# Moving part of the attention epilogue of a hybrid decoder layer between VectorE, ScalarE and TensorE

## The chip, the core and the metric

The kernel runs on one core of a Trainium2 chip. The metric is device time in microseconds (us) of one execution; lower is better. Three executions of the kernel before were timed, and one more was taken with the hardware profiler. The engines are named PE (TensorE), ACT (ScalarE), DVE (VectorE), POOL (GpSimd) and SP (SyncE, which here only issues transfers).

## The reference

A decoder layer over a sequence of 1024 tokens with model width 1024 computes a SwiGLU half-step, then a mixing step, then a second SwiGLU half-step, all with RMS norms before and after and with shift, scale and gate taken from a conditioning vector. The change lies in the mixing step, cut here to what matters:

```python
attn = sliding_window_attention(q, k, v, sinks)        # 8 query heads, 2 key heads, window 128
    # scores + bias; m = max(scores, sink); p = exp(scores - m)
    # p = p / (sum(p) + exp(sink - m));  out = p @ v
ssm = s5_ssm(u, ...)                                   # diagonal complex state space model, GELU, GLU
mixed = concat([rms_norm(attn, g_attn_out), rms_norm(ssm, g_ssm_out)])
mixed = mixed @ w_out
x = x + ga2 * rms_norm(mixed, g_post_mix)
```

The norm of attention's output needs, for each token, the sum of the squares of its 512 attention columns. It is a scale of the token's row, so it can be applied after the product with w_out.

## The kernel before, in words

Everything is float32. A large product is written as three TensorE products of rounded halves: `split` (lines 69 and 70) makes a high half with a ScalarE copy and a low half with a VectorE subtraction, and `mm3` (lines 74 to 76) adds high*high, high*low and low*high into one PSUM bank. So nearly every operand that PE reads in a `mm3` has passed through ACT first and DVE second.

The mixing step (`mix`) treats the tokens in 8 tiles of 128. For attention, tile t passes through three functions that are called one step apart. `at(n)` calls `at_values(n - 3)`, then `at_turn(n - 2)`, then `at_scores(n)`.

- `at_scores(t)`: 16 score products per tile on PE (line 841); 8 fused add, maximum and store operations on DVE, one per head (line 851); 8 exponentials on ACT with their sums (line 860); the reciprocal of the sums on DVE (lines 861, 862); and 8 scalings of the 128x256 probabilities by that reciprocal on DVE (line 864).
- `at_turn(t)`: 16 transposes on PE (line 875) into four PSUM banks, each split into halves (lines 69, 70 by way of line 877).
- `at_values(t)`: the products with v (lines 74 to 76, by way of line 889), their squares on ACT into the tile `sq` (line 890), and copies of the output on ACT (line 892). DVE then sums the four squares of a column (line 894), one PE product with a column of ones sums over the partitions (line 896), and DVE copies the result into one column of `ss_a` (line 897).

After the last tile (in `more`, line 1057) `rstd_a` is made from `ss_a` through a short chain on DVE and ACT (lines 141 to 145, 151), and the attention output and attention's share of w_out are split (lines 740 and 741 for w_out, which come through the stream `late`). `out_a(t)` multiplies tile t by attention's share of w_out in two halves of 512 columns and scales each half by `rstd_a` on DVE as it leaves PSUM (line 1048). In between stand the four quarters of the state space model: `ss_state(q)` (lines 978 to 1005; its two scans are lines 992 and 993, and half of its last products run on POOL) and `ss_out(q)` (lines 1016 to 1029).

PSUM has eight banks. The mixing step gives them out in turn (`mb`), in the order in which the program is written, so that a function's bank becomes free only when its user of eight allocations before has been read out.

The order of the instructions on each engine is not the order of the text. A planner in the framework goes through the program at build time with estimates of its own for what each operation takes, and puts on each engine's queue what is ready then, earlier text first. Only the long loops of the two SwiGLU half-steps have an order that is written out by hand (`pinned`). On the chip each engine takes its own queue in that order.

Of the kernel before, what the change touches and what calls it, by code (L numbers as in the profile page):

```python
# [15 lines left out]
MUL, ADD, SUB, MAX, MIN = ALU.mult, ALU.add, ALU.subtract, ALU.max, ALU.min  # L16

P = 128
# [12 lines left out]
def tile_layer(ctx: ExitStack, tc: tile.TileContext, a: dict, out: bass.AP, stage: str = "all"):  # L31
    nc = tc.nc
    pe, act, dve, pool, sp = nc.tensor, nc.scalar, nc.vector, nc.gpsimd, nc.sync
# [10 lines left out]
    def slot(tag, shape, dt=F32):  # L44
        uid[0] += 1
        return sb.tile([P] + list(shape), dt, tag=tag, name=f"{tag}_{uid[0]}")

    def bank(tag, shape=(512,)):
        uid[0] += 1
        return ps.tile([P] + list(shape), F32, tag=tag, name=f"{tag}_{uid[0]}")  # L50

    def small(n, name):
        uid[0] += 1
        return sm.tile([P, n], F32, tag=f"s_{name}_{n}", name=f"s{uid[0]}")
# [10 lines left out]
    def names(c, *idx):  # L65
        return tuple(f"{c}{i}" for i in idx)
# [5 lines left out]
    def mm3(psum, wh, wl, xh, xl, first, last, goes_on=False):  # L72

        pe.matmul(psum, wh, xh, start=first, stop=False, skip_group_check=goes_on)  # L74
        pe.matmul(psum, wh, xl, start=False, stop=False, skip_group_check=goes_on)  # L75
        pe.matmul(psum, wl, xh, start=False, stop=last, skip_group_check=goes_on)  # L76
# [26 lines left out]
    ones = cp.tile([P, 2], F32, name="ones")  # L103
# [6 lines left out]
    rstd_a, rstd_s, ss_a = (cp.tile([P, 8], F32, name=x) for x in ("rstd_a", "rstd_s", "ss_a"))  # L110
# [600 lines left out]

    AT = (1, 1, 0, 1, 0, 1, 0, 1, 0, 1, 0, 1)


    mb = Rot(*names("b", *range(8)))

# [47 lines left out]
    def mix(hm, st, st_u, late, shares, todo, start):  # L764
# [65 lines left out]
        def at_scores(t):  # L830
            nk = 1 if t == 0 else 2
            p2 = [slot(x, [2, 2, 256]) for x in (("a26", "a27"), ("a17", "c0"))[t % 2]]
            pr = {4 * kv + m: p2[m // 2][:, kv, m % 2] for kv in range(2) for m in range(4)}
            mx = small(8, "mx")
            ks = slice((2 - nk) * P, 256)
            for mp in range(2):
                pb = [bank(mb(), [2, 256]) for _ in range(2)]
                for m in (2 * mp, 2 * mp + 1):
                    for kv in range(2):
                        rows = slice(64 * kv, 64 * kv + 64)  # L840
                        pe.matmul(  # L841
                            pb[kv][:, m % 2, ks],
                            qT[m][rows, t * P : (t + 1) * P],
                            kT[rows, (t + 1 - nk) * P : (t + 1) * P],
                            start=True,
                            stop=True,
                        )
                for kv in range(2):
                    for m in (2 * mp, 2 * mp + 1):
                        hd = 4 * kv + m  # L850
                        dve.tensor_tensor_reduce(
                            pr[hd][:, ks], pb[kv][:, m % 2, ks], bias[kv][:, m, ks], 1.0, sink[:, hd : hd + 1],
                            ADD, MAX, mx[:, hd : hd + 1],
                        )
            nm, sm_, es = small(8, "nm"), small(8, "sum"), small(8, "es")
            dve.tensor_scalar(nm, mx, -1.0, None, op0=MUL)
            dve.tensor_tensor(es, sink, mx, op=SUB)
            act.activation(es, es, AF.Exp)
            for hd in range(NH):
                act.activation(pr[hd][:, ks], pr[hd][:, ks], AF.Exp, bias=nm[:, hd : hd + 1], accum_out=sm_[:, hd : hd + 1])  # L860
            dve.tensor_tensor(sm_, sm_, es, op=ADD)
            dve.reciprocal(sm_, sm_)
            for hd in range(NH):
                dve.tensor_scalar(pr[hd][:, ks], pr[hd][:, ks], sm_[:, hd : hd + 1], None, op0=MUL)
            A[t] = pr

        def at_turn(t):
# [11 lines left out]
        def at_values(t):  # L879
            nk = 1 if t == 0 else 2  # L880
            pr = A.pop(t)
            tk = slice(t * P, (t + 1) * P)
            sq = slot("t0", [4, P])
            for kv in range(2):
                rows = slice(64 * kv, 64 * kv + 64)
                po = bank(mb(), [4, P])
                for b in range(2 - nk, 2):
                    vb = t - 1 + b
                    mm3(po.rearrange("p m q -> p (m q)"), v_hi[:, vb, :], v_lo[:, vb, :], *pr[kv, b], b == 2 - nk, b == 1)
                act.activation(sq[rows], po[rows], AF.Square)  # L890
                for m in range(4):
                    act.copy(ag[m][rows, tk], po[rows, m, :])
            s1 = slot("t1", [P])
            dve.tensor_reduce(s1, sq.rearrange("p m q -> p q m"), op=ADD, axis=mybir.AxisListType.X)
            pc = bank(mb(), [2])
            pe.matmul(pc[:, 0:1], s1, ones[:, 0:1], start=True, stop=True)
            dve.tensor_copy(ss_a[:, t : t + 1], pc[:, 0:1])

        def ss_load(q):
# [13 lines left out]
        def at(n):  # L913

            if 3 <= n < NT + 3:
                at_values(n - 3)
            if 2 <= n < NT + 2:
                at_turn(n - 2)
            if n < NT:
                at_scores(n)  # L920
# [117 lines left out]
        acc = []  # L1038

        def out_a(t):  # L1040
            acc.append(slot(("r1", "r2", "r3", "a8", "c0", "a4", "a5", "a6")[t], [D]))
            tk = slice(t * P, (t + 1) * P)
            for dh in range(2):
                dk = slice(dh * 512, dh * 512 + 512)
                pb = bank(mb())
                for m in range(4):
                    mm3(pb, mix_a[0][m][:, tk], mix_a[1][m][:, tk], wo[m][0][:, dk], wo[m][1][:, dk], m == 0, m == 3)
                dve.tensor_scalar(acc[t][:, dk], pb, rstd_a[:, t : t + 1], None, op0=MUL)  # L1048

        wo, mix_a = [], []  # L1050

# [25 lines left out]
        while n < NT + 3:  # L1077
            n = more(n)
        ss_state(3)
        out_a(0)  # L1080
        out_a(1)
        ss_out(2)
        y_split(0)
        y_split(1)
        out_a(2)
        out_a(3)
        ss_out(3)
# [16 lines left out]
        for m in range(4):  # L1104
            gh, gl = late.get(4 + m)
            for hf in range(2):
                tk = slice(hf * 512, hf * 512 + 512)
                pb = bank(mb())
# [617 lines left out]
```

## Time and profile before

| what | us |
|---|---|
| median of the three timed executions | 1684.39 |
| lowest and highest of them | 1682.94 and 1687.2 |
| the profiled execution: its own time | 1682.71 |
| the profiled execution: its span, first to last instruction | 1680.9 |
| mixing step, attention and state space model, about | 740 to 960 of the span |

The mean granted clock of PE over the span is 0.993 of full speed. In the rows below, busy time is time in which the engine executes; an idle time in square brackets stands before the row's first instruction, with the engine, tile and line that ended it. Names such as `h` or `a` are the program's slots without their number; `b` are the PSUM banks.

### The profile page before, as it was taken

The numbers are of one execution on the slowest core, as the hardware profiler recorded it, in microseconds if no ns is written. First come the engines' busy times: TensorE is split into PE (matmuls) and PEld (weight loads), VectorE is DVE, ScalarE is ACT, GpSimd is POOL, SyncE is SP. The second block draws the span as 40 slices with busy tenths as digits, with TensorE's granted clock in tenths as the row PEclk, the third lists the DMA queues.
The fourth block names the chain that finished last, engine by engine and source line by source line (L and its number), as shares of the span: only waits on it lengthen the run. The fifth ranks groups of instructions, "written<-read, shape, count | busy, mean of one in ns | idle before, by whom it ended". The sixth has DMA issues, their size and how long they took to land.

```text
span 1680.9 us, 22023 instructions
## 1 busy us (share of the span) xinstructions
PE 1642.0 (98%) x7669; PEld 1349.3 (80%) x7669; DVE 1245.1 (74%) x2359; ACT 803.1 (48%) x1642; POOL 69.2 (4%) x119
## 2 busy tenths in 40 slices
PE   5999999999999999999989999999999999999998
PEld 4888888877788888888767887888888888888886
DVE  7999997889869768755589387777665666679585
ACT  5633333553345458736574268533333333355462
POOL 0011100001100000000013000000000000000000
PEclk8999999999999999999989999999999999999999
DMA  9176752234496334530232135352322233493344
GB/s 381 47 277 230 250 191 95 98 141 153 135 319 238 118 117 156 193 113 13 93 97 76 63 113 189 105 181 96 107 94 94 101 125 105 168 360 113 107 135 141
DMA packets 111056, 249.07 MB, mean 148 GB/s; under 512 B 11976, under 2 KB 27632, under 8 KB 110944
## 3 DMA queue, kind: packets, MB, share of 16 engines
q1 hardware_dynamic: 101216, 214.12, 36.9%
q0 software_dynamic: 9152, 32.49, 5.7%
q8 instruction: 60, 0.98, 0.2%
q10 hardware_dynamic: 576, 1.05, 0.2%
q14 instruction: 52, 0.43, 0.1%
HBM read 187.87 MB, written 59.75 MB: 147 GB/s over the span
## 4 chain that ended last, share of the span: by engine, by line
PE 89%; DVE 7%; ACT 2%; issue 1%; DMA 1%; SPq 0%; DVEq 0%; ACTq 0%
PE b L76 27%; PE b L75 27%; PE b L74 27%; PE b L841 1%; PE b L929 1%; PE b L931 1%; PE b L930 1%; PE b L875 1%; DVE h L495 1%; DVE w L70 1%; PE b L1020 0%; DVE h L532 0%; DVE a L166 0%; PE b L207 0%; ACT q L1431 0%
## 5 line engine op out<-in xcount | busy, mean ns | idle before, releaser
L75 PE MATMUL b<-a,w 128*128 128x512 f32 x1260 | 492.0, 390 | 3.4 <-DVE a L70 3.4
L76 PE MATMUL b<-a,w 128*128 128x512 f32 x1260 | 492.2, 391 | 1.0 <-DVE w L70 0.8
L74 PE MATMUL b<-a,w 128*128 128x512 f32 x1260 | 488.8, 391 | 3.9 <-ACT h L536 2.2
L74 PEld LDWEIGHTS b<-a,w 128*128 128x128 f32 x1260 | 236.9, 188 | 56.5 <-ACT h L536 3.8
L75 PEld LDWEIGHTS b<-a,w 128*128 128x128 f32 x1260 | 237.1, 188 | 52.5 <-DVE a L70 3.8
L76 PEld LDWEIGHTS b<-a,w 128*128 128x128 f32 x1260 | 237.1, 188 | 51.9 <-DVE w L70 3.0
L70 DVE TENSOR_TENSOR w<-r,w 128x512 fp32r<-128x512 f32 (+1 forms) x208 | 144.1, 694 | 129.9 <-ACT w L69 129.6
L75 PE MATMUL b<-w,r 128*128 128x512 f32 x528 | 205.5, 389 | 0.0
L76 PE MATMUL b<-w,r 128*128 128x512 f32 x528 | 205.4, 389 | 0.0
L74 PE MATMUL b<-w,r 128*128 128x512 f32 x528 | 183.5, 389 | 0.0
L69 ACT CAST w<-r 128x512 fp32r<-128x512 f32 (+1 forms) x208 | 129.1, 623 | 95.0 <-DVE r L397 82.4
L69 ACT CAST r<-a 128x512 fp32r<-128x512 f32 x110 | 68.5, 623 | 144.9 <-PE b L76 105.8
L70 DVE TENSOR_TENSOR r<-a,r 128x512 fp32r<-128x512 f32 x110 | 75.8, 689 | 73.6 <-ACT r L69 73.3
L74 PEld LDWEIGHTS b<-w,r 128*128 128x128 f32 x528 | 99.1, 188 | 20.7
L75 PEld LDWEIGHTS b<-w,r 128*128 128x128 f32 x528 | 99.1, 188 | 20.7 <-DVE w L70 0.2
L76 PEld LDWEIGHTS b<-w,r 128*128 128x128 f32 x528 | 99.1, 188 | 20.5
L69 ACT CAST w<-t 128x512 fp32r<-128x512 f32 (+1 forms) x114 | 69.9, 613 | 78.8 <-DVE t L400 32.3
L70 DVE TENSOR_TENSOR w<-t,w 128x512 fp32r<-128x512 f32 (+1 forms) x114 | 77.8, 682 | 34.4 <-ACT w L69 34.4
L532 DVE TENSOR_TENSOR h<-h,b 128x512 f32<-128x512 f32 x120 | 82.2, 685 | 20.4 <-PE b L76 18.6
L520 ACT ACTIVATE h<-h 128x512 f32<-128x512 f32 x60 | 38.0, 633 | 117.8 <-DVE h L532 117.8
L70 DVE TENSOR_TENSOR w<-a,w 128x512 fp32r<-128x512 f32 x110 | 75.3, 684 | 0.0
L74 PE MATMUL b<-a,a 128*128 128x512 f32 x182 | 71.3, 395 | 0.8 <-DVE r L1048 0.7
(393 smaller groups left out, 2475.2 us busy)
## 6 DMA issues: line engine op xcount, KB each, us to landing
r<-in_w_gu SPq DMA_DIRECT2D x87, 512.0 KB, 4.2
g_d<-h SPq DMA_DIRECT2D x154, 256.0 KB, 2.1
a<-g_d SPq DMA_DIRECT2D x110, 256.0 KB, 2.8
q<-in_w_ada POOLq DMA_DIRECT2D x48, 512.0 KB, 4.6
a<-in_w_d SPq DMA_DIRECT2D x88, 256.0 KB, 5.4
a<-in_w_ada SPq DMA_DIRECT2D x24, 512.0 KB, 9.6
a<-in_x SPq DMA_DIRECT2D x12, 512.0 KB, 6.1
x_d<-a SPq DMA_DIRECT2D x12, 512.0 KB, 3.5
```

Of the source, the lines that this page charges most:

```text
L69: act.copy(hi, src)
L70: eng.tensor_tensor(lo, src, hi.bitcast(F32), op=SUB)
L74: pe.matmul(psum, wh, xh, start=first, stop=False, skip_group_check=goes_on)
L75: pe.matmul(psum, wh, xl, start=False, stop=False, skip_group_check=goes_on)
L76: pe.matmul(psum, wl, xh, start=False, stop=last, skip_group_check=goes_on)
L495: dve.tensor_tensor(d, x, y, op=op)
L520: act.activation(dst, src, AF.Silu)
L532: dve.tensor_tensor(dst, dst, pb, op=ADD)
L841: pe.matmul(pb[kv][:, m % 2, ks], qT[m][rows, t * P : (t + 1) * P], kT[rows, (t + 1 - nk) * P : (t + 1) * P], start=True, stop=True,)
L875: pe.transpose(pt[:, m, :], pr[4 * kv + m][:, b * P : (b + 1) * P], ident)
L929: pe.matmul(pb, hh, wh, start=k == 0, stop=False)
L930: pe.matmul(pb, hh, wl, start=False, stop=False)
```

## The change

There are three edits. For the last two attention tiles (6 and 7) the 8 scalings of the probabilities are issued on ACT and not on DVE. For the same two tiles the DVE sum over the four squares is gone: PE takes the four 128x128 blocks of `sq` itself, in four products with the column of ones that add up in one bank. And in `out_a`, for all eight tiles, the first half of 512 columns (dh = 0) is scaled by `rstd_a` on ACT; the second half stays on DVE.

```diff
+    LATE = 6
...
             for hd in range(NH):
-                dve.tensor_scalar(pr[hd][:, ks], pr[hd][:, ks], sm_[:, hd : hd + 1], None, op0=MUL)
+                if t < LATE:
+                    dve.tensor_scalar(pr[hd][:, ks], pr[hd][:, ks], sm_[:, hd : hd + 1], None, op0=MUL)
+                else:
+                    act.mul(pr[hd][:, ks], pr[hd][:, ks], sm_[:, hd : hd + 1])
...
-            s1 = slot("t1", [P])
-            dve.tensor_reduce(s1, sq.rearrange("p m q -> p q m"), op=ADD, axis=mybir.AxisListType.X)
             pc = bank(mb(), [2])
-            pe.matmul(pc[:, 0:1], s1, ones[:, 0:1], start=True, stop=True)
+            if t < LATE:
+                s1 = slot("t1", [P])
+                dve.tensor_reduce(s1, sq.rearrange("p m q -> p q m"), op=ADD, axis=mybir.AxisListType.X)
+                pe.matmul(pc[:, 0:1], s1, ones[:, 0:1], start=True, stop=True)
+            else:
+                for m in range(4):
+                    pe.matmul(pc[:, 0:1], sq[:, m, :], ones[:, 0:1], start=m == 0, stop=m == 3)
...
-                dve.tensor_scalar(acc[t][:, dk], pb, rstd_a[:, t : t + 1], None, op0=MUL)
+                if dh:
+                    dve.tensor_scalar(acc[t][:, dk], pb, rstd_a[:, t : t + 1], None, op0=MUL)
+                else:
+                    act.mul(acc[t][:, dk], pb, rstd_a[:, t : t + 1])
```

## Rows read from the trace of the kernel before

**Rows 1.** The page's first part: busy time, share of the span, instructions.

```profile
PE 1642.0 (98%) x7669; PEld 1349.3 (80%) x7669; DVE 1245.1 (74%) x2359; ACT 803.1 (48%) x1642; POOL 69.2 (4%) x119
```

**Rows 2.** Busy time by stretch; after POOL: PE's granted clock, DMA share, GB/s.

```profile
850.00:860.00 10.00, 10.00 (x80) 7.11 (x77) 7.41 (x28) 6.25 (x21) 0.00 (x0) 1.00 0.01 5
860.00:870.00 10.00, 6.57 (x44) 4.54 (x42) 10.00 (x19) 9.86 (x33) 1.54 (x1) 0.86 0.46 155
870.00:880.00 10.00, 8.65 (x30) 6.39 (x31) 10.00 (x22) 3.75 (x12) 4.46 (x5) 0.62 0.29 93
880.00:890.00 10.00, 10.00 (x64) 7.97 (x64) 9.78 (x14) 6.38 (x11) 0.93 (x3) 1.00 0.18 47
...
910.00:920.00 10.00, 9.26 (x68) 7.50 (x67) 10.00 (x17) 1.96 (x3) 4.02 (x5) 1.00 0.01 2
...
1020.00:1050.00 30.00, 26.27 (x129) 20.64 (x128) 20.34 (x43) 27.55 (x50) 0.00 (x0) 1.00 0.54 192
```

**Rows 3.** Timeline of PE: start, us, engine, line, then idle time before it.

```profile
863.94 0.66 PE L875 MATMUL b<-ident,a 128*128 128x128 f32 x4
865.46 0.38 PE L896 MATMUL b<-ones,t 128*128 128x1 f32 x2 [0.86 <-DVE t L894]
867.78 0.80 PE L74 MATMUL b<-h,a 128*128 128x512 f32 x1 [1.94 <-ACT h L69]
868.75 0.79 PE L74 MATMUL b<-h,a 128*128 128x512 f32 x1 [0.18 <-ACT h L69]
871.35 0.80 PE L75 MATMUL b<-h,a 128*128 128x512 f32 x1 [1.80 <-DVE h L70]
...
918.70 0.50 PE L74 MATMUL b<-a,a 128*128 128x512 f32 x1 [0.74 <-DVE r L1048]
```

**Rows 4.** Single microseconds: length, PE busy, PE's granted clock, DMA share, GB/s.

```profile
866.00:867.00 1.00, 0.00 (x0) 1.00 0.98 389
867.00:868.00 1.00, 0.22 (x1) 0.64 0.86 344
...
877.00:878.00 1.00, 1.00 (x6) 0.74 0.00 0
```

**Rows 5.** The chain that ended last, in order of time.

```profile
852.25 0.31 PE b L896 x2
...
859.40 1.93 DVE a L864 x7
...
868.90 1.19 DVE s L861
```

**Rows 6.** Timeline of ACT, columns as in Rows 3.

```profile
854.92 0.58 ACT L69 CAST h<-b 128x512 fp32r<-128x512 f32 x1
859.25 1.15 ACT L740 ACTIVATE a<-a,cols 128x1024 fp32r<-128x1024 f32 x1 [3.75 <-DVE s L851]
...
866.53 0.49 ACT L860 ACTIVATE c<-c,s 128x256 f32<-128x256 f32 x1
866.93 0.18 ACT L860 ACTIVATION_READ_ACCUMULATOR c<-c,s 128x1 f32 x1
867.14 2.05 ACT L69 CAST h<-b 128x512 fp32r<-128x512 f32 x4
...
918.03 1.28 ACT L1023 ACT_TABLE_LOAD   x1 [11.18 <-PE b L1020]
```

**Rows 7.** Timeline of DVE, columns as in Rows 3.

```profile
857.66 0.19 DVE L862 RECIPROCAL s<-s 128x8 f32<-128x8 f32 x1
...
871.22 0.18 DVE L862 RECIPROCAL s<-s 128x8 f32<-128x8 f32 x1
...
893.18 1.07 DVE L894 TENSOR_REDUCE t<-t 128x128 f32<-128x512 f32 x1 [1.85 <-ACT t L890]
```

**Rows 8.** Instructions of lines 894 and 1048: shortest, median, longest (ns), first and last start.

```profile
L894 DVE TENSOR_REDUCE t<-t x8: 1020/1042/1070, 779.2 to 893.2; 128x128 f32<-128x512 f32 x8
...
L1048 DVE TENSOR_SCALAR a<-b,rstd_a x8: 750/750/751, 928.1 to 958.7; 128x512 f32<-128x512 f32 x8
```

## The prediction

> **What bounds the kernel now.** I read the busy shares first. PE is busy for 98% of the span and no other engine for more than 74% [rows 1], so work taken from DVE or given to ACT counts only where it moves a moment at which PE stands still, or where PE's own work grows.
>
> Next I split the mixing step into stretches of 10 us, to find those moments [rows 2]. From 850 to 860 PE is full at clock 1.00. From 860 to 880 it is not: 3.43 and 1.35 us idle, at granted clocks of 0.86 and 0.62, while DVE is busy for all 20 us. From 880 PE is full again, except for one gap of 0.74 us between 910 and 920. So there is one hole here, at 864 to 878, and one pinhole.
>
> PE's timeline says what the hole waits for [rows 3]. PE ends tile 6's transposes at about 864.6; it then waits 0.86 us for tile 5's sum of squares (line 894), 1.94 and 0.18 us for the high halves of tile 6's probabilities (line 69 on ACT), and 1.80 us for the first low half (line 70 on DVE). That is 4.78 us, until 871.35. Reading single microseconds [rows 4], the clock is still 1.00 in the idle microsecond 866 to 867, changes inside 867 to 868 (mean 0.64), and is back during 877 to 878 (mean 0.74). Its lower level of 1.2 GHz thus holds until about 877.5; from 871.35 that is 6.15 us of busy PE at half of 2.4 GHz, or 3.1 us lost on top of the wait.
>
> The chain of waits runs through DVE up to 871.35, and tile 6's scalings stand in it with 1.93 us for seven of the eight [rows 5]. On ACT the same stretch is a different picture [rows 6]: idle for 3.75 us up to 859.25, then in one run through w_out's first scaling (line 740), tile 5's read-out, tile 7's exponentials and, last, tile 6's four casts, which start only at 867.14 although the transposes were done by 864.6. Both engines are therefore close to setting the end of the hole.
>
> **The change, part by part.** The sum is made against the profiled execution's 1682.71 us and carried to the median, 1684.39, which is 1.68 above it.
>
> *Tile 6's scalings.* DVE loses 8 x 0.276 = 2.2 us (1.93 over seven) [rows 5]. ACT gains eight operations on 128x256; the trace has none of the kind, and the nearest are the exponentials of that size, which step by 0.40 us up to the readback of the sum, and by about 0.5 with it, as the exponential lasts [rows 6]. A plain multiplication has no readback, so I take 0.40, 3.2 us in all, and keep 4.1 (8 x 0.51, a cast of twice the size) as the upper end. The scalings can start when the reciprocal is done, at 857.85 [rows 7], inside ACT's idle time, and would end at 861.05. Of their 3.2 us, 1.40 lie in the hole up to 859.25 and 1.8 push what follows. Queued behind them on ACT are line 740, tile 5's read-out, tile 7's exponentials and tile 6's casts; PE waits for the last. Line 740 (1.15 us) got its place only because ACT had nothing else; nothing of it is needed in this stretch, and I let it fall behind. Then the casts start 0.65 later, at 867.8, the first is done at 868.3 (four in 2.05 us), and the first low half needs DVE for about 0.6 more. DVE, 2.2 us ahead, reaches that place at about 868.4 rather than 870.6, so PE goes on at about 869.0, not at 871.35: **-2.4 us**. If line 740 keeps its place, casts at 868.95 give 870.1: -1.2. The lower level of the clock is left as it was, since the wait still lasts over 4 us.
>
> The Trainium skill, "ScalarE: Activation LUTs", section "Rules for kernel authors", speaks against this edit: a multiplication belongs on VectorE, not on ScalarE. The rows agree about the price (0.276 against 0.40 us), but DVE is the full engine here and ACT had 3.75 us free; by the rule alone the edit would lose 8 x 0.12 = 1 us, which I don't count.
>
> *Tile 7's scalings.* Another 2.2 us leave DVE after 871.22 [rows 7], where PE has queued work, and 3.2 us go to ACT. I cost them at nothing if they run behind tile 6's casts: between 870 and 880 ACT is busy for only 3.75 of 10 us [rows 2]. If that cover is gone, because they are queued ahead of the casts, the casts come 3.2 us later; that is the first rival.
>
> *Sums of squares.* Two reductions of 1.04 us [rows 8] leave DVE, as does its 1.85 us of waiting ahead of the last [rows 7]. PE issues eight products where it had two. One takes 0.31 us with its two passes [rows 5], so six more are **+1.9 us**, and PE is full between 880 and 900, where these two lines fall: this is on the path. The lower end is 0, if some of them fall into a wait. Behind them on PE stands tile 7's product with v; what they wait for, the second square of line 890, is ready before the reduction was. `sq` is now released by PE rather than DVE, so tile 7's squares on ACT could wait for tile 6's four products, which come before tile 7's product with v anyway: nothing.
>
> *Half of attention's share.* Eight scalings of 0.75 us [rows 8], 6.0 us, leave DVE; ACT gets eight reads of 128x512 from PSUM, at 0.51 each by the casts [rows 6], 4.1 us. Most lie between 918 and 960, where PE is the bound; nothing. The one place where they count is the pinhole: at 918.70 PE had waited 0.74 us for line 1048 to free a bank [rows 3]. With DVE some 6 us freer by then and two engines emptying banks, I take that away: **-0.7 us** (ends -0.7 and +0.7, if an ACT multiplication, waiting for `rstd_a`, holds up the table load and GELU behind it; ACT had stood idle for 11.18 us before them [rows 6]).
>
> No transfer is added or moved in the text; SP's and POOL's queues keep their order, except as the planner shifts them. Sum: -2.4 + 1.9 - 0.7 = **-1.2 us**, 1681.5 for the profiled execution, 1683.2 on the median.
>
> **The rivals.**
>
> *ScalarE takes DVE's place in the hole (slower).* Tile 7's scalings are earlier in the text than tile 6's casts. If tile 7's sums are ready while ACT still reads out tile 5, the planner puts all 3.2 us ahead of the casts. Then the casts start at 867.8 + 3.2 = 871.0, PE goes on at 872.1, 0.8 later than before; with +1.9 and -0.7 that is +2.0. With line 740 in its place and 0.51 us per scaling it is +5. For it: ACT is 9.86 of 10 us busy there [rows 2]. Against it: tile 7's reciprocal stood well behind its exponentials, at 871.22, because DVE was full. It decides from the point at which ACT has more than 3.2 - 1.4 us of new work ahead of the casts. About 1686.4, up to 1689.4.
>
> *The hole closes enough that the clock doesn't fall (faster).* The change to the lower level came after 2.8 us of nearly idle PE. If the waits shrink by 2.4 us and the level stays, 3.1 us more come back: -2.4 - 3.1 + 1.9 - 0.7 = -4.3; if PE finds no wait at all, -4.8 - 3.1 + 1.9 - 0.7 = -6.7. For it: both engines' queues are shuffled here, and DVE has 11 us less to do by 920. Against it: tile 7's exponentials alone, 4 us on ACT, fill the wait. About 1677.7 to 1680.1. The Trainium skill, "TensorE: Matmul & The Clock Gate", section "HAM oscillation — how this bites in real kernels", says that waits of PE bring the low clock and that work kept contiguous avoids it; rows 4 show the low clock following the wait.
>
> *The planner's order moves elsewhere.* Engine times before 930 change, so later choices can. Between 1020 and 1050 PE has 3.73 us idle under an ACT that is 92% busy [rows 2]; closed, the total is -4.9. A new hole of the kind at 864, wait and clock, costs 7.9: +6.7, or 1691.1.
>
> *It does nothing where it aims.* The hole is set by what neither edit touches (exponentials, POOL's share); then only the products remain, +1.9 - 0.7 = +1.2. I count it with the forecast, since it can't be told from it in time.
>
> **How the numbers follow.** A measurement of this kernel can tell about 0.3%, or 5 us. Forecast 0.32 (0.30 of it within the bound, 0.02 faster); ScalarE in DVE's place 0.22 (0.13 within, 0.09 slower); the clock held 0.28 (0.22 faster, 0.06 within); the planner elsewhere 0.18 (0.05 faster, 0.05 within, 0.08 slower). Faster 0.29, same 0.54, slower 0.17. The range goes from the hole quite closed, 1677, to the worst of ScalarE, 1689; a new hole lies outside. The forecast's own range is 1681 to 1686.
>
> **What would show it.** Right: ACT's eight scalings of tile 6 begin at the reciprocal, without idle time ahead of them; tile 6's casts come before tile 7's scalings; PE's wait after the transposes ends about 2.4 us earlier against them; line 896's successors take eight products of 0.31 us; no wait at the first read-out of `out_a`. Wrong: a wait of PE for ACT where it was for DVE, longer than 4.8 us; a granted clock of 1.00 through the stretch; or any difference of over 2 us outside 850 to 930.

## The result and the profile after

The changed kernel is slower: 1695.52 us at the median of six runs (1691.84 to 1695.78) against 1684.24 for six runs of the kernel before beside them, a ratio of 1.0056 with a 95% interval of 1.0044 to 1.0067. The forecast, 1683.2, was 12 us too low, and the time lies outside the range of 1677 to 1689. The profiled execution took 1695.78 us, with a span of 1694.0.

The line numbers have moved: 864 is now 869 (ACT) or 866 (DVE), 860 is 862, 862 (the reciprocal) is 864, 875 is 880, 890 is 895, 892 is 897, 894 is 901, 896 is 902 (tiles 0 to 5) and 905 (the products on the squares), 740 is 742, 978 is 987, 1016 is 1025, 1020 is 1029 and 1048 is 1060 (ACT) or 1058 (DVE). Each experiment's kernel has numbers of its own, a few lines on.

First the busy shares, the page's first part, of the kernel after:

```profile
PE 1653.8 (98%) x7681; PEld 1360.4 (80%) x7681; DVE 1232.8 (73%) x2333; ACT 814.2 (48%) x1666; POOL 74.9 (4%) x119
```

DVE and ACT exchanged their work as planned. PE has 12 instructions more and is busy for 11.8 us more than in [rows 1]; 12 records of about a quarter of a microsecond can't do that. Either PE did something else, or it did the same things more slowly. Busy time by stretches of 10 us of the kernel after (columns as in [rows 2], so the number after POOL is PE's granted clock) says which:

```profile
860.00:870.00 10.00, 5.95 (x46) 4.95 (x44) 9.96 (x17) 9.98 (x35) 4.48 (x2) 0.95 0.33 106
870.00:880.00 10.00, 7.79 (x28) 5.91 (x26) 10.00 (x17) 8.47 (x20) 2.53 (x4) 0.50 0.36 122
880.00:890.00 10.00, 10.00 (x44) 7.84 (x43) 6.53 (x9) 4.90 (x11) 5.29 (x4) 0.69 0.27 90
890.00:900.00 10.00, 10.00 (x49) 7.68 (x48) 2.84 (x6) 2.57 (x6) 0.17 (x3) 0.66 0.39 104
900.00:910.00 10.00, 10.00 (x75) 8.16 (x74) 7.11 (x10) 8.33 (x17) 0.00 (x0) 0.83 0.12 30
910.00:920.00 10.00, 10.00 (x72) 8.51 (x72) 10.00 (x12) 3.65 (x6) 9.53 (x7) 0.83 0.48 131
```

From 880 to 920 PE doesn't stand still for a moment, where before the pinhole was, but its clock is 0.69, 0.66, 0.83 and 0.83 where it was 1.00 [rows 2]. Single microseconds of the kernel after (PE alone: busy, granted clock) place the falls:

```profile
868.00:869.00 1.00, 0.15 (x2) 1.00 0.96 365
869.00:870.00 1.00, 1.00 (x13) 0.54 0.25 98
...
886.00:887.00 1.00, 1.00 (x7) 0.93 0.26 37
892.00:893.00 1.00, 1.00 (x7) 0.98 0.00 0
893.00:894.00 1.00, 1.00 (x5) 0.50 0.01 2
899.00:900.00 1.00, 1.00 (x4) 0.60 0.78 315
...
906.00:907.00 1.00, 1.00 (x12) 0.81 0.30 16
...
913.00:914.00 1.00, 1.00 (x17) 0.77 0.57 145
```

Divided between 2.4 and 1.2 GHz, these means give three stretches at 1.2 GHz in the mixing step: 869.1 to 886.1, 893.0 to 899.8 and 906.6 to 913.5, where the kernel before had one, 867.3 to 877.5 [rows 4]. A fourth, 1043.2 to 1046.6, lies in the second half-step. PE's timeline of the kernel after shows what stands ahead of each (x8 is four products of two passes each):

```profile
863.11 1.69 PE L880 MATMUL b<-ident,a 128*128 128x128 f32 x14
868.85 1.79 PE L987 MATMUL b<-a,q 128*64 128x128 f32 x16 [4.05 <-ACT r L897]
872.85 0.59 PE L902 MATMUL b<-ones,t 128*128 128x1 f32 x2 [2.21 <-DVE t L901]
...
876.00 0.63 PE L1025 MATMUL b<-q,a 128*128 128x128 f32 x2
...
881.46 0.79 PE L74 MATMUL b<-h,a 128*128 128x512 f32 x1
...
890.08 1.05 PE L905 MATMUL b<-ones,t 128*128 128x1 f32 x8
...
892.95 1.22 PE L1029 MATMUL b<-q,a 64*128 64x128 f32 x4
...
905.43 0.95 PE L905 MATMUL b<-ones,t 128*128 128x1 f32 x8
```

Ahead of the first fall stands one wait of 4.05 us, for ACT, and a second one of 2.21 us, for DVE, stands inside it. Ahead of the other two stands no wait at all: each begins at most 2 us behind four of the new one-column products, among small products of the state space model (lines 1025 and 1029).

The wait for ACT comes from ACT's queue. First two lines of ACT's timeline of the kernel before, tile 5's read-out:

```profile
860.38 0.59 ACT L890 ACTIVATE t<-b 64x512 f32<-64x512 f32 x1
...
862.21 0.75 ACT L892 COPY r<-b 64x128 f32<-64x128 f32 x4
```

And ACT's timeline of the kernel after:

```profile
859.31 3.31 ACT L869 ACTIVATE a<-a,s 128x256 f32<-128x256 f32 x8 [2.45 <-DVE s L864]
862.52 1.13 ACT L742 ACTIVATE a<-a,cols 128x1024 fp32r<-128x1024 f32 x1
863.56 0.49 ACT L862 ACTIVATE a<-a,s 128x256 f32<-128x256 f32 x1
...
867.60 0.57 ACT L895 ACTIVATE t<-b 64x512 f32<-64x512 f32 x1
...
869.31 0.75 ACT L897 COPY r<-b 64x128 f32<-64x128 f32 x4
870.09 2.05 ACT L69 CAST h<-b 128x512 fp32r<-128x512 f32 x4
...
874.09 0.92 ACT L869 ACTIVATE a<-a,s 128x256 f32<-128x256 f32 x2
```

Tile 6's scalings begin with tile 6's reciprocal, as forecast, and take 0.40 us each. But behind them tile 7's exponentials go first, from 863.56, and tile 5's read-out has moved from 860.38 to 867.60 (1.36 of these 7.2 us stand between the two profiles already ahead of it: tile 4's sum of squares is at 852.18 and 853.54). `at_scores(7)` is called one step before `at_values(5)`, so it is the earlier text. That the planner took it first because ACT now came free late enough for both to be ready is argued from the text's order; the planner's own estimates aren't on record. The read-out frees the PSUM bank that the products of `ss_state(1)` want (line 987), and feeds the reduction that the one-column products of tile 5 wait for.

The difference can be added up from the single microseconds. I call the part of PE's busy time that the clock costs "lost": busy time times (1 - granted clock), summed over the microseconds.

| profiled execution | span | PE busy | PE idle ahead of 780 | PE idle, 840 to 1120 | lost, 840 to 1120 |
|---|---|---|---|---|---|
| before | 1680.9 | 1642.0 | 20.6 | 9.6 | 3.9 |
| after | 1694.0 | 1653.8 | 21.9 | 9.6 | 15.8 |

The idle time between 840 and 1120 is the same: the mixing step has 0.7 more, and the stage behind it 0.7 less. Of the 13.1 us between the spans 1.3 are idle time ahead of 780, where PE's order is the same in both kernels, so the change can't be given them; the other 11.8 are busy time. The six added products take about 1.4 of these (from their start to that of the next product 0.98 and 0.88 us, against 0.15 and 0.31 for the single ones), which leaves some 10.4 for the clock. The rise in "lost" is 11.9, somewhat too high: it takes a product at half the clock to last twice as long, where in these timelines one of 512 columns steps by 0.43 us instead of 0.23, and four passes of line 1029 by 1.15 instead of 0.64. The fourth stretch has 1.5 of the 15.8.

The six timed executions say the same without a trace: four took 1695.5 to 1695.8 us at a mean granted clock of 0.986, two 1691.8 and 1692.0 at 0.988. It is one program, with one order.

### The profile page after: what moved, and what is told of

Read it like the earlier page. It is cut to its first block, busy times and chain, and to the rows that moved or that the text cites. A ratio compares the mean times of both kernels' runs of the same rounds, so it can differ in the third digit from the quotient of the medians.

```text
span 1694.0 us, 22052 instructions
## 1 busy us (share of the span) xinstructions
PE 1653.8 (98%) x7681; PEld 1360.4 (80%) x7681; DVE 1232.8 (73%) x2333; ACT 814.2 (48%) x1666; POOL 74.9 (4%) x119
## 4 chain that ended last, share of the span: by engine, by line
PE 87%; DVE 6%; ACT 4%; DMA 1%; issue 1%; SPq 0%; DVEq 0%; ACTq 0%
PE b L74 26%; PE b L76 26%; PE b L75 26%; PE b L1029 1%; PE b L843 1%; PE b L938 1%; PE b L940 1%; PE b L939 1%; PE b L1025 1%; PE b L880 1%; DVE w L70 1%; PE b L207 1%; DVE h L495 0%; DVE h L532 0%; DMA a<-x_d 0%
## 5 line engine op out<-in xcount | busy, mean ns | idle before, releaser
L75 PEld LDWEIGHTS b<-w,r 128*128 128x128 f32 x528 | 99.1, 188 | 20.6
L76 PEld LDWEIGHTS b<-w,r 128*128 128x128 f32 x528 | 99.1, 188 | 20.6
L69 ACT CAST w<-a 128x512 fp32r<-128x512 f32 x110 | 67.8, 617 | 8.3 <-PE b L76 6.1
```

Source lines behind the costliest of these rows:

```text
L69: act.copy(hi, src)
```

## The experiments

No kernel leaves out a part of the computation; those with "unread products" add some whose results nobody uses. All ratios are to runs of the kernel before on the same chip. "The scalings", "the squares" and "the share" are the three edits.

### Each edit alone

Only the scalings:

```diff
-                dve.tensor_scalar(pr[hd][:, ks], pr[hd][:, ks], sm_[:, hd : hd + 1], None, op0=MUL)
+                if t < LATE:
+                    dve.tensor_scalar(pr[hd][:, ks], pr[hd][:, ks], sm_[:, hd : hd + 1], None, op0=MUL)
+                else:
+                    act.mul(pr[hd][:, ks], pr[hd][:, ks], sm_[:, hd : hd + 1])
```

> Only the scalings of tiles 6 and 7 go to ScalarE; squares and w_out's scaling stay as before. Theory A (ScalarE's longer queue lengthens TensorE's wait in the hole at 864, and the low clock with it): 5 to 9 us slower than before, idle time of TensorE between 864 and 875 about 6 us as in the changed kernel, low clock for over 15 us. Theory B (the low clock of the changed kernel comes from the one-column products, which give TensorE too little to do): only the 1.5 us of longer wait, so 1 to 3 us slower, and the low clock lasts about 10 us as before.

Measured: 1694.06 us, ratio 1.0049 (1.0036 to 1.0062). PE's waits in its timeline:

```profile
867.37 1.98 PE L983 MATMUL b<-a,q 128*64 128x128 f32 x16 [4.05 <-ACT r L897]
871.37 0.59 PE L901 MATMUL b<-ones,t 128*128 128x1 f32 x2 [2.02 <-DVE t L899]
```

Two stretches of 10 us of the same run:

```profile
870.00:880.00 10.00, 8.63 (x27) 6.71 (x27) 10.00 (x16) 7.03 (x17) 1.14 (x3) 0.50 0.45 157
...
890.00:900.00 10.00, 10.00 (x75) 7.48 (x74) 1.97 (x4) 4.14 (x13) 0.79 (x4) 1.00 0.42 107
```

The same wait of 4.05 us and a low clock to 884 are there; the falls at 893 and 906 are not. This edit makes the hole worse, and the later falls are another's. This profile has, besides, two low stretches in the second half-step, 6.8 us from 1037.6, behind a wait of 3.11 us, and 3.4 us from 1058.1: 4.9 of its 12.2 us lost between 840 and 1120, where the change has 1.5. So the edits don't simply add up: the scalings alone cost nearly as much as all three together.

Only the squares:

```diff
-            dve.tensor_reduce(s1, sq.rearrange("p m q -> p q m"), op=ADD, axis=mybir.AxisListType.X)
-            pe.matmul(pc[:, 0:1], s1, ones[:, 0:1], start=True, stop=True)
...
+            else:
+                for m in range(4):
+                    pe.matmul(pc[:, 0:1], sq[:, m, :], ones[:, 0:1], start=m == 0, stop=m == 3)
```

> Only the sums of squares of tiles 6 and 7 go to TensorE. Theory A: six more products of 0.25 us, 1.5 us slower than before (0.5 to 3), the clock falls once, near 867, as before. Theory B: 5 to 8 us slower, and the granted clock falls again to about half behind the one-column products, twice after 885.

Measured: 1686.48 us, ratio 1.0018 (1.0005 to 1.0031), from 12 runs that don't agree with each other: seven at 1685.5 to 1686.5, two at 1690 to 1691, three at 1693 to 1695.5. The profile is of one of the last; a stretch of it:

```profile
890.00:900.00 10.00, 10.00 (x54) 7.83 (x56) 3.62 (x6) 3.12 (x9) 4.61 (x7) 0.69 0.53 156
```

With PE full, its clock fell at 886, 3 us behind the first eight one-column passes; 4.8 of this profile's 13.9 us lost lie in the second half-step. The mean granted clock of each run fits: 0.993 to 0.995 in the seven, 0.987 to 0.989 in the other five. One program, in one order, is 4 to 10 us slower when its clock is lower, which speaks for the clock as a cost of its own.

Only the share:

```diff
-                dve.tensor_scalar(acc[t][:, dk], pb, rstd_a[:, t : t + 1], None, op0=MUL)
+                if dh:
+                    dve.tensor_scalar(acc[t][:, dk], pb, rstd_a[:, t : t + 1], None, op0=MUL)
+                else:
+                    act.mul(acc[t][:, dk], pb, rstd_a[:, t : t + 1])
```

> Only half of w_out's scalings go to ScalarE. The planned order of TensorE is that of before, instruction for instruction. Both theories: no difference (0.7 us faster to 0.7 us slower); the wait of 0.74 us at 918 is gone or shorter. A third theory C (ScalarE's eight multiplications out of PSUM hold up the GELU behind them): 2 us slower or more.

Measured: 1684.81 us, ratio 0.9995 (0.9986 to 1.0004). PE's wait at 918 is gone and the rest as before, PE's order instruction for instruction.

### The one-column products

Of the change, the squares alone, with 128 columns of ones in place of one:

```diff
-                    pe.matmul(pc[:, 0:1], sq[:, m, :], ones[:, 0:1], start=m == 0, stop=m == 3)
+                    pe.matmul(pc, sq[:, m, :], WIDE[0], start=m == 0, stop=m == 3)
```

> The sums of squares alone, as in e2, but each of TensorE's eight products reads 128 columns of ones instead of one column (same sums, 128 times over; about the same 0.25 us each). If the one-column products bring the second fall of the clock (theory B), it goes: clock 1.00 from 880 to 920, executions of 1690 us and more become as rare as before (e2 had 5 of 12), median 1685 to 1687. If the order around them does it, and not how little they keep TensorE busy, the spread of e2 stays: 4 to 6 of 12 at 1690 or more.

Measured: 1689.48 us, ratio 1.0012 (1.0001 to 1.0022), with the kernel before at 1687.12 beside it. By the expectation's own count, 4 of 12 at 1690 or more, it came out as the second case had it; but 3 of the 23 runs of the kernel before lay there too, and the four had a mean clock of 0.989 to 0.992, not the 0.987 to 0.989 of the one-column ones. The stretch where the one-column run had 0.69:

```profile
890.00:900.00 10.00, 10.00 (x96) 7.96 (x97) 8.80 (x11) 7.64 (x17) 5.00 (x5) 1.00 0.58 160
```

The trace has no fall there, but since most runs with one column had none either, by their times, the two can't be told apart. The same edit in the whole change, whose order on PE is otherwise the same, is the better test:

> The whole change with 128 columns of ones in place of one column, as in e4. The planned order of TensorE is that of the change. If the one-column products bring the falls at 892 and 906 (theory B): both gone, low clock of 16 to 18 us in the stretch 860 to 920 instead of 30.7, and 4 to 8 us faster than the change, near e1's 1694 or below. Rival: the falls stay where they were, no gain.

Measured: 1689.32 us (1687.18 to 1691.66), ratio 1.0018 (1.0008 to 1.0029); the change's interval lies wholly above it. Stretches of this run:

```profile
890.00:900.00 10.00, 10.00 (x74) 7.57 (x74) 3.39 (x7) 5.12 (x15) 0.17 (x3) 1.00 0.41 107
900.00:910.00 10.00, 10.00 (x97) 8.63 (x97) 10.00 (x12) 7.62 (x12) 4.14 (x2) 1.00 0.35 84
```

The same work, with products 128 columns wide, takes 6.2 us less: the falls at 893 and 906 are gone, and 7.0 us of lost time with them (15.8 to 8.8 between 840 and 1120). So in this order the falls hung on those products being one column wide. The scalings, which alone cost 1.0049, are in this run too: what they cost isn't the same in every order.

### The order of the queues

The whole change, with tile 7's softmax moved behind `at_values(5)` in the text, so that the read-out comes first:

```diff
+            if n == 8:
+                at_soft(7)
             if 2 <= n < NT + 2:
```

> The whole change, with the exponentials of tile 7 moved in the text behind tile 5's read-out, so that ScalarE's queue has the first half of the read-out ahead of them. Theory A (order on ScalarE: the exponentials hold up tile 5's read-out, which frees the bank that TensorE waits for): the wait of 4.05 us at 865 shrinks by 2 us or more, and the total falls by 2 to 6 us against the change as given. Rival (ScalarE's sheer load of 3.2 us more ahead of tile 6's casts): the wait only moves to the casts, the total stays within 2 us of the change as given.

Measured: 1702.04 us, ratio 1.0095 (1.008 to 1.011), the slowest of all. PE's waits:

```profile
870.31 0.59 PE L910 MATMUL b<-ones,t 128*128 128x1 f32 x2 [4.70 <-DVE t L909]
873.13 0.77 PE L1035 MATMUL b<-q,a 128*128 128x128 f32 x2 [2.23 <-DVE a L1008]
```

The wait for ACT is gone, and as long a one for DVE has taken its place. DVE's timeline, tile 5's reduction in the change and in this run:

```profile
871.81 0.98 DVE L901 TENSOR_REDUCE t<-t 128x128 f32<-128x512 f32 x1
...
869.23 1.03 DVE L909 TENSOR_REDUCE t<-t 128x128 f32<-128x512 f32 x1
```

The reduction did come 2.6 us earlier, and PE's two waits are 6.9 us together, against 6.3. What grew is the low clock: 41 us in the mixing step, where the change has 30.7. Neither theory's number held: giving the read-out its place back moved the waits and didn't keep the clock up.

The kernel before, with tile 7's softmax behind tile 6's transposes:

```diff
                 at_turn(n - 2)
+            if n == 8:
+                at_soft(7)
```

> The kernel before with one move alone: the softmax of tile 7 stands behind tile 6's transposes in the text, so that ScalarE casts tile 6 ahead of or between tile 7's exponentials. No work changes engine. If ScalarE's order sets the hole (theory A), TensorE's wait at 864 to 871 shrinks from 4.8 us by 2 to 3.5 us, and the kernel is 2 to 7 us faster than before, the more if the clock doesn't fall. If VectorE's full queue sets it (the reading the change rests on), no gain: within 1.5 us of before.

Measured: 1694.13 us, ratio 1.0043 (1.0029 to 1.0058), outside both theories. Of its six waits, all on DVE, the longest:

```profile
875.51 0.80 PE L75 MATMUL b<-h,a 128*128 128x512 f32 x1 [2.71 <-DVE h L70]
```

The same with tile 7's scalings and the share on ACT:

> e6, and tile 7's scalings and half of w_out's scalings go to ScalarE as in the change (tile 6's scalings and the sums of squares stay on VectorE). Theory A: at least as fast as e6, 3 to 8 us faster than before, since ScalarE has room only after tile 6's casts. Theory C (any scaling on ScalarE costs): slower than e6 by 2 us or more.

Measured: 1690.13 us, ratio 1.0023 (1.0014 to 1.0032): better, still slower than before, with the clock low from 869 to 889. Freeing ACT's queue moves the hole to DVE.

### Which tile's scalings

Tile 6's alone (`if t == 6`):

> Only tile 6's scalings go to ScalarE. If these are what lengthens ScalarE's queue ahead of tile 5's read-out and tile 6's casts: as e1, 5 to 10 us slower than before, with the wait of 4 us for the bank and about 17 us of low clock. Rival (tile 7's scalings, which stand behind, do it): within 2 us of before.

Measured: 1689.36 us, ratio 1.0016 (1.0004 to 1.0027), 12 runs from 1684.81 to 1693.02. Tile 7's alone (`if t == 7`):

> Only tile 7's scalings go to ScalarE. The first waits of the hole, up to 871, are those of before. If tile 6's scalings do the harm: within 2 us of before. Rival: 4 us slower or more, through a second fall of the clock behind tile 7's later transposes.

Measured: 1685.61 us, ratio 0.9999 (0.999 to 1.0008). PE's first wait in the hole, in its timeline, with tile 6's scalings on ACT:

```profile
868.53 1.97 PE L983 MATMUL b<-a,q 128*64 128x128 f32 x16 [4.04 <-ACT r L897]
```

And with tile 7's:

```profile
867.18 0.38 PE L901 MATMUL b<-ones,t 128*128 128x1 f32 x2 [0.85 <-DVE t L899]
```

Tile 6's scalings alone turn the order on ACT and make the wait of 4 us; tile 7's alone cost nothing. In the profiled execution of tile 6's the clock stayed low to 888.8 and lost 10.2 us over the table's stretch, but the loss over all runs, 2.7 us, is smaller than I expected. Both tiles' together had cost 1.0049, more than 1.0016 and 0.9999 give. The pair's profile has 3.4 us more lost in the second half-step than this one; why, no run shows.

### Filling the hole

If the low clock is a cost of its own and not merely a companion of the wait, work that nobody reads should gain time. In these kernels the order of the unread products and of tile 5's one-column products is written out by hand (`pinned`). First in the kernel before:

```diff
+                if t == 6 and kv == 0:
+                    spare = v_hi[:, 0:4, :].rearrange("p t q -> p (t q)")
+                    for _ in range(20):
+                        pinned(lambda: pe.matmul(po.rearrange("p m q -> p (m q)"), v_hi[:, 0, :], spare, start=True, stop=True))
```

> The kernel before, with 20 products of 512 columns that nobody reads put on TensorE between tile 5's sum of squares and tile 6's product with v, into the bank that this product then starts afresh: some 4.6 us of work in a hole of 4 us or more, no other work added or moved. If the low clock is what the hole costs beyond the wait (theory A), the clock stays at 1.00 through 860 to 880 and the kernel is 2 to 4 us faster than before. Rival: the clock falls all the same, or it doesn't matter for the end (VectorE's queue sets the next waits): no change, or 1 to 4 us slower, since the extra products then run at the low clock.

Measured: 1684.46 us against 1686.69, ratio 0.9991 (0.9981 to 1.0001). PE's timeline:

```profile
866.68 4.81 PE L892 MATMUL b<-a 128*128 128x512 f32 x20
...
874.77 0.49 PE L75 MATMUL b<-h,a 128*128 128x512 f32 x1 [1.70 <-DVE h L70]
```

The two stretches of the hole in the same run:

```profile
860.00:870.00 10.00, 9.14 (x60) 7.46 (x61) 10.00 (x24) 9.62 (x32) 0.57 (x1) 1.00 0.48 157
870.00:880.00 10.00, 8.30 (x43) 6.26 (x41) 10.00 (x20) 4.75 (x13) 5.42 (x5) 1.00 0.23 61
```

The clock stays at 1.00 throughout, so the 3.9 us lost before are back, and the 20 products, longer than the wait that they fill, eat much of it: too small an effect to be told from none. Then 18 such products in the whole change, ahead of the 4.05 us wait, once with wide ones and once without:

> The whole change with 128 columns of ones and with 18 products of 128x512 that nobody reads ahead of ss_state(1)'s products, which waited 4.05 us on ACT in the change; 18 at the 0.23 us between starts that the unread products showed are 4.1 us, so they take the place of a wait and the last eight transposes follow them. Theory (the low clock behind the hole is the cost that is left): the clock stays at 1.00 or falls for under 10 us, the 7.3 us lost at the low level in the run with 128 columns of ones go, and the time is 1682 to 1686. Rival (the waits and the planner's new order are the cost, the clock only goes along): the clock stays up but the time stays at 1688 to 1692.

> The whole change, its one-column products too, with the same 18 unread products. Theory: only the low clock behind the hole goes (the falls behind the eight one-column products each stay), so 5 to 8 us off the change: 1687.5 to 1690.5, and slower than the run with both edits. Rival (once the hole is filled, the falls later are gone too, since they came of the hole and not of the one-column products): as the run with both, 1682 to 1686.

Measured: 1690.84 us, ratio 1.0024 (1.001 to 1.0039), and 1690.82, ratio 1.0019 (1.0003 to 1.0036), with the kernel before at 1686.85. (Three of those 23 runs of the kernel before took 1695 to 1696 us, at a mean clock of 0.987 to 0.988 where the others have 0.991 to 0.993: it, too, can be as slow as the change.) PE's timeline of the first:

```profile
863.53 4.36 PE L903 MATMUL b<-a 128*128 128x512 f32 x18
...
872.93 0.59 PE L907 MATMUL b<-ones,t 128*128 128x1 f32 x2 [2.87 <-DVE t L906]
```

The first wait was filled, but the second remained, and at its end, at 872, the clock fell all the same and stayed low to 885. So the first told nothing on the question. In the second, with one-column products, the time is 0.3 us above what the theory gave and no slower than the first; in its profile the falls behind those products are gone too. Its second eight passes, in PE's timeline, and the stretch around them:

```profile
901.44 0.95 PE L910 MATMUL b<-ones,t 128*128 128x1 f32 x8
...
900.00:910.00 10.00, 9.37 (x84) 7.60 (x85) 10.00 (x9) 7.21 (x9) 7.05 (x7) 1.00 0.40 86
```

Products of 512 columns follow its first eight passes, at 892, but these second ones stand among small products from 897 to 906, much as in the change, and the clock stays up. One-column products alone don't bring a fall, then, nor do small ones beside them suffice. What decides in a given execution stays open. With three more unread products, which read tile 5's squares and so lie in the second wait:

```diff
+                for _ in range(3):
+                    pinned(lambda: pe.matmul(pc, ident, sq.rearrange("p m q -> p (m q)"), start=True, stop=True))
```

> The run with wide ones and 18 unread products, with three more unread products of 128x512 in plain float32 that read tile 5's squares, between ss_state(1)'s products and tile 5's one-column products: they lie where that run still had a 2.87 us wait on DVE, at the end of which the clock fell and stayed low for 13.6 us (6.3 us lost). Theory (the low clock is a cost of its own): with both waits filled the clock stays at 1.00 through 850 to 960 and the time is 1683 to 1687, 4 to 7 us below that run and no slower than the kernel before by over 0.15%. Rival (the order and the waits are the cost): the clock stays up, but the time stays at 1689 to 1692.

Measured: 1685.01 us against 1684.94, ratio 1.0004 (0.9994 to 1.0015). PE's timeline:

```profile
863.16 4.36 PE L903 MATMUL b<-a 128*128 128x512 f32 x18
...
869.58 2.84 PE L905 MATMUL b<-t,ident 128*128 128x512 f32 x6
872.58 0.38 PE L909 MATMUL b<-ones,t 128*128 128x1 f32 x2
```

Two stretches of the same run:

```profile
870.00:880.00 10.00, 9.33 (x46) 6.04 (x45) 10.00 (x16) 8.66 (x20) 2.46 (x5) 1.00 0.31 107
880.00:890.00 10.00, 10.00 (x64) 7.86 (x63) 7.54 (x12) 6.96 (x14) 7.06 (x7) 1.00 0.44 124
```

Tile 5's one-column products come at 872.58, 0.35 us earlier than without the three, so the wait's end has hardly moved; the clock is 1.00 from 850 to 960, and the profiled span is 6.1 us shorter (1689.7 to 1683.6). All three edits stand in this kernel, with some 7 us of useless products, and it takes as long as the kernel before. With the runs of one program that differ by their clock, this shows the clock as a cost of its own. Three limits: the two runs' intervals still overlap between 1.001 and 1.0015, the planner's order behind the hole differs a little, and four of the 12 runs took 1688.4 to 1689.8 us at a mean clock of 0.992 (the others 0.994 to 0.997), so the filling doesn't keep the clock up in every execution. The Trainium skill, "TensorE: Matmul & The Clock Gate", section "HAM oscillation — how this bites in real kernels", has it that a wait of PE brings the low clock to the work behind it, and that products kept together keep the clock up; the hole agrees, with 0.50 and 0.69 between 870 and 890 in the change and 1.00 with both waits filled.

Last, the two edits of the kernel before that cost nothing alone, the 20 unread products and the share:

> The kernel before with the 20 unread products in the hole, and with half of attention's share of w_out scaled on ACT: the two edits that cost nothing by themselves (0.9991 and 0.9995). Theory: 1 to 3 us below the kernel before, a ratio of 0.998 to 0.9995. Rival (both save what the planner loses elsewhere): within 1 us of it.

Measured: 1682.57 us against 1684.94, ratio 0.9988 (0.998 to 0.9997). Of the fifteen versions it is the only one whose interval lies below the kernel before, by 0.12%; with so many versions tried, and an end at 0.9997, that is weak.

## Why the prediction was wrong

**What bounds the kernel** was read right as far as it went: the hole at 864 to 878 and the pinhole at 918 were the places where PE stood still, and work taken from DVE elsewhere (the share, or tile 7's scalings by themselves) made no difference, as costed. But two of the change's three costly places, 893 and 906, lie where PE never stands still. The 3.1 us lost left out the 1.6 us of products before 871.35, which ran at the low level too; the table has 3.9. And DVE's full 20 us aren't all work: line 861's addition over 8 columns, 0.15 us at 856.18, took 1.27 at 868.82, on the chain [rows 5], and ended with a product on POOL (870.07). What held it isn't shown.

**Tile 6's scalings, -2.4.** The price was right (3.31 us for eight) and the place too, at the reciprocal and inside ACT's idle time; ACT's idle time ahead of them, 2.45 us, is about what the sum left there (3.75 less 1.40), though the list of signs had none. Two choices behind them failed. "Line 740 ... I let it fall behind": it kept its place at 862.52. And "queued behind them on ACT are line 740, tile 5's read-out, tile 7's exponentials and tile 6's casts" took the old order for granted. Tile 7's exponentials went ahead of tile 5's read-out, so PE stopped at the products of `ss_state(1)`, which no term of the sum mentioned. The term came to about +0.7 us, PE's extra idle time in the mixing step.

**"The lower level of the clock is left as it was, since the wait still lasts over 4 us"** is the step that made the miss large. I had priced a change of the low stretch only on the side of a gain, in the second rival, at 3.1 us, and on the side of a loss only for a new hole. Unforeseen was that it can stay low far longer behind much the same idle time: to 886.1 where it was 877.5, 17 us and not 10. In the kernel before, mostly products of 512 columns ran from 871.35 to 876 at the lower level; in the change, 5.5 us of small products of the state space model (lines 1025 and 1029) stood in that place, and the clock came back only behind the next 512-column ones. That this is why it stayed low is argued from the two timelines; no run varied it alone, and the cause stays open.

**The squares, +1.9.** Somewhat too high in itself: six more products cost 1.4 us, since a pass of one column takes about 0.13 us in a row and not 0.155. The larger part had no term: two falls of the clock with PE busy all the time, 7.0 us of lost time, which the run with wide ones took away with 6.2 us of the total.

**Half of attention's share, -0.7.** The wait at 918 went, as forecast; alone the edit can't be told from no change, as it should be. A scaling on ACT took 0.68 to 0.70 us and not 0.51, and nothing waited for it.

**The rivals.** ScalarE did take DVE's place, but not by the way described: it was not tile 7's scalings ahead of the casts (they ran behind them, at 874.09), but tile 7's exponentials ahead of tile 5's read-out. Its price, up to +5, had no clock in it. "A new hole ..., wait and clock", +6.7, was nearest in kind, and the 0.08 that it had on the slower side too little. The 11 us that DVE was to have less by 920 don't come out of the terms: 2.2 twice and 2.1 make 6.5, and the share's 6.0 fall behind 918. Of the signs of error one half is in the trace, a wait of PE for ACT where it was for DVE; at 4.05 us it isn't longer than 4.8 us. Of the signs of being right, the casts ahead of tile 7's scalings and the wait at 918 came true and didn't save the forecast.

## What to carry to other kernels

Where a wait of PE already brings its clock down, price an edit there by the low stretch behind the wait as well, in both directions. What kind of products runs in it may matter. When a queue is filled by a planner from what is ready, an operation put into an engine's idle time can reorder what stands behind it: ask for each follower who comes first once both are ready, and who waits for the one that loses. A sum over partitions as a product with one column can cost TensorE more than its own time: two falls of the clock stood behind such products here, and none where the right side was wider, at 0.1 us more per four.

## What the runs showed of the hardware

- PE's clock fell with PE busy in every microsecond, at 893 and 906, behind one-column products among small ones. With 128 columns of ones it stayed at 1.00, and the kernel was 6.2 us faster. The same passes among small products, at 901 in the run with 18 unread products, brought no fall.
- PE lost no time by doing more: with wide ones the changed kernel took 1.0018 of the kernel before, with 21 unread products in its waits besides, 7.2 us of them, 1.0004; the intervals overlap.
- Runs of one and the same program differ by whether a fall happens: the squares alone gave 1685.5 to 1686.5 in seven runs, at a mean clock of 0.993 to 0.995, and up to 1695.43, at 0.987, in the others.
